# A hybrid decoder block on one core: Strassen operands paired in 1024-column tiles, a fifth raw buffer, and both norms' statistics and transposes reordered

## The chip, the cores and the metric

The kernel runs on one core of one Trainium2 chip. The metric is the device time of one execution in microseconds (us); the median of several runs counts. Four engines compute: TensorE (PE, with its weight loads written PEld), VectorE (DVE), ScalarE (ACT) and GpSimd (POOL). SyncE (SP) issues most of the DMAs. Each engine works through its own instructions in order; semaphores hold an instruction back until its inputs are there.

## The reference, cut to what matters

One layer of a decoder with 256 tokens, 2048 channels and a feed-forward width of 5632, all in float32:

```
mix = token_mixers(x, ...)                  # one input projection, gated linear attention,
                                            # forgetting attention, merge, output projection
x   = layer_norm(ALPHA*x + mix, ln1_g, ln1_b)
g   = causal_dwconv(x @ w_gate, conv_w, conv_b)
x   = layer_norm(ALPHA*x + (gelu(g) * (x @ w_up)) @ w_down, ln2_g, ln2_b)
x   = x + sigmoid(x @ w_ple_gate) * (p @ w_ple_proj)
```

The layer norm takes mean and variance over the 2048 channels of each token. The input spreads make the two norms' gains and biases about three times as wide as usual; that changes no operation.

## The kernel before, in words

**Weights.** All large weights come through one array, in units of 128 partitions x 2048 columns (1 MB), 284 in all. A unit is loaded as two "raw" tiles of 1024 columns (512 KB) by SP, into four raw buffers used in turn. Because TensorE multiplies in the shorter float32r format, each raw tile is split: ACT copies it to a "hi" tile, DVE subtracts to get the "lo" tile, and the product is summed from three matmuls (hi x hi, lo x hi, hi x lo, the activations being split likewise). There is a ring of six hi and one of six lo buffers. `unit()` (line 152) hands out the next unit and prepares up to three ahead; `prep()` (line 133) makes the loads and the splits.

**Order.** PE's and SP's order is the program's where the code says so; the order on DVE, ACT and POOL is set by a scheduler from priorities (`tc.high_priority`) and from when it expects inputs.

**The stages.** Input projections with attention beside them; the output projection with the residual and the first norm (`residual`, `end1`); gate and up projections with the convolution; the down projection `down` with the second norm (`end2`); the last gate (`begin2` and after).

**Down projection (dn).** It runs in two halves of 1024 output columns. Each half has 22 units, each a pair of 128-row weight blocks. Fourteen are "classic": 24 matmuls of 512 columns. Eight are done by a Strassen scheme (`strassen`, line 1079): seven products instead of eight, 21 matmuls. Their operands are the blocks b11, b21, b22 and four sums T1 = b12 - b11, T3 = b12 - b22, T2 = b22 - T1, T4 = b21 - T2 on DVE, each split into hi and lo (`prep_s`, line 110). b11 and each T get a hi and a lo tile of their own, 512 columns wide (`split512`); the second raw tile is split whole. So a Strassen unit takes six buffers of each ring, a classic unit two. They alternate through most of each half. A Strassen unit's products use them in the order b11, b21, b22, T1, T3, T2, T4. `fold` adds the product banks to the residual z when a half's Strassen units are done. At the end of a half `ev` adds the four result banks to z and takes the statistics of each 512-column group (bn_stats).

**The norms.** `ln_steps` (line 755) gives three steps for a half t of the tokens (128 each): `stat` (mean and rstd, with one power on POOL), `norm(g)` and `turn(g)` for each of four 512-column groups g. Groups 0 and 2 (`AFF_DVE`) have gain and bias applied by two DVE operations in `norm`, and `turn` transposes on PE and splits. Groups 1 and 3 are only normalised on ACT in `norm`; `turn` transposes, then applies gain and bias in four 128-column pieces, two on ACT and two on DVE, and then splits. For these groups the residual stream z itself gets gain and bias later, by `affine`, beside the next stage. `end1` interleaves by hand on PE: the last matmuls of the output projection, transposes, the first half of the per-layer-embedding projection (`proj`, whose result `put` copies and POOL stores), and the first three gate/up units (`phase0` with token half 0, `phase1` with half 1). `end2` does the same with the second half of that projection.

```
            tail_mm(1, 1, 0)
            turn0(0)
            tail_mm(1, 1, 1)
            stat1()
```

is the place in `end2` (lines 1147 to 1150) where the first transpose of the second norm stands. POOL's DMAs (two stores of z1, four of the embedding projection, two more) use a scratch of 8192 bytes for their descriptors.

Of the kernel before, what the change touches and what calls it, by code (L numbers as in the profile page):

```python
# [9 lines left out]
F32 = mybir.dt.float32  # L10
# [9 lines left out]
P = 128  # L20
# [13 lines left out]
P_STAT = 5000  # L34
P_LN1 = (2000, 2000)
P_LN2 = (4000, 1000)
# [6 lines left out]
            (0, 1, 2, 4, 3, 6, 5, 9, 7, 11, 8, 14, 10, 16, 12, 19, 13, 15, 17, 18, 20, 21))  # L43
AFF_DVE = (0, 2)
LN_ORDER = (1, 0, 3, 2)
# [7 lines left out]
def tile_block(ctx: ExitStack, tc: tile.TileContext, wu, wfv, wpp, xT_in, x_in, pT_in, wlr,  # L53
# [28 lines left out]
    def copy(o, i, scale=1.0):  # L82
        nc.scalar.activation(o, i, AF.Copy, bias=0.0, scale=scale)  # L83

# [17 lines left out]

    def split512(src, name):
        hi = ring.tile([P, 512], F32R, tag="hi", name=f"{name}h")
        copy(hi, src)
        lo = ring.tile([P, 512], F32R, tag="lo", name=f"{name}l")
        nc.vector.tensor_tensor(lo, src, hi.bitcast(F32), ALU.subtract)
        return hi, lo

    def prep_s(u):  # L110

        r0, r1 = [ring.tile([P, 1024], F32, tag="raw", bufs=4, name=f"raw{u}_{h}")
                  for h in range(2)]
        for h, r in enumerate((r0, r1)):
            nc.sync.dma_start(r, wu[u, :, h * 1024:(h + 1) * 1024])
        b12, b11, b22, b21 = r0[:, 0:512], r0[:, 512:1024], r1[:, 0:512], r1[:, 512:1024]
        ops = [split512(b11, f"b11_{u}")]
        hi = ring.tile([P, 1024], F32R, tag="hi", name=f"hi{u}_1")
        copy(hi, r1)
        lo = ring.tile([P, 1024], F32R, tag="lo", name=f"lo{u}_1")  # L120
        nc.vector.tensor_tensor(lo, r1, hi.bitcast(F32), ALU.subtract)
        ops += [(hi[:, 512:1024], lo[:, 512:1024]), (hi[:, 0:512], lo[:, 0:512])]
        ts = {}
        for n, a, b in (("T1", b12, b11), ("T3", b12, b22), ("T2", b22, "T1"),
                        ("T4", b21, "T2")):
            ts[n] = t2(f"{n}_{u}")
            nc.vector.tensor_tensor(ts[n], a, ts.get(b, b) if isinstance(b, str) else b,
                                    ALU.subtract)
        for n in ("T1", "T3", "T2", "T4"):
            ops.append(split512(ts[n], f"{n}_{u}"))  # L130
        ready[u] = ops

    def prep():
        u = n_prep[0]
        n_prep[0] += 1
        if u in dn_s:
            prep_s(u)
            return
        his, los = [], []
        for h in range(2):  # L140
            raw = ring.tile([P, 1024], F32, tag="raw", bufs=4, name=f"raw{u}_{h}")
# [4 lines left out]
            nc.vector.tensor_tensor(lo, raw, hi.bitcast(F32), ALU.subtract)  # L146
            his.append(hi)
            los.append(lo)
        ready[u] = (his, los)
# [45 lines left out]
    def load_consts2():  # L195
        nc.sync.dma_start(gnb, gnorm.broadcast_to([P, 512]))
        for i in range(2):
            maskf = ring.tile([P, 4, 256], F32, tag="raw", bufs=4, name=f"maskf{i}")
# [122 lines left out]
    def fv_prep(u, hs=(0, 1), his=None, los=None):  # L321
        his, los = his or [], los or []
        for h in hs:
            raw = ring.tile([P, NS], F32, tag="raw", bufs=4, name=f"fvraw{u}_{h}")
# [429 lines left out]

    def ln_steps(zof, stats, t, act_out, gb_, cg, cb, nm, prio):

# [11 lines left out]
        def norm(g):  # L768
            e = slice(g * 512, g * 512 + 512)
            zc = zof(t, g)  # L770
            with tc.high_priority(prio):
                if g in AFF_DVE:
                    nc.vector.scalar_tensor_tensor(zc, zc, mv[:, 0:1], gb_[0][:, e],
                                                   ALU.subtract, ALU.mult)
                    nc.vector.scalar_tensor_tensor(zc, zc, mv[:, 3:4], gb_[1][:, e],
                                                   ALU.mult, ALU.add)
                else:
                    nc.scalar.activation(zc, zc, AF.Identity, scale=mv[:, 3:4], bias=mv[:, 4:5])

        def turn(g):  # L780
            zc = zof(t, g)
            with tc.high_priority(prio):
                pt = mxtile(f"pt{nm}{t}{g}")
                for i in range(4):
                    nc.tensor.transpose(pt[:, i * P:i * P + P], zc[:, i * P:i * P + P], ident)
                if g in AFF_DVE:
                    split_T(pt, act_out[g], t)
                    return
                y = t2("lny").rearrange("p (k t) -> p k t", t=P)
                for i in range(4):  # L790
                    kt = 4 * g + i
                    gc, bc = chn[:, cg + kt:cg + kt + 1], chn[:, cb + kt:cb + kt + 1]
                    src = pt[:, i * P:i * P + P]
                    if i % 2 == 0:
                        nc.scalar.activation(y[:, i, :], src, AF.Identity, scale=gc, bias=bc)
                    else:
                        nc.vector.tensor_scalar(y[:, i, :], src, gc, bc, ALU.mult, ALU.add)
# [18 lines left out]

    def affine(zof, gb_, after, gs=range(4)):
        for t in range(2):
            for g in gs:
                zc = zof(t, g)  # L820
# [12 lines left out]
    def ple_prep(half):  # L833
# [4 lines left out]
        for k in range(2):  # L838
            raw = ring.tile([P, 1024], F32, tag="raw", bufs=4, name=f"praw{half}{k}")
            nc.sync.dma_start(raw, wpp[half, :, k * 1024:k * 1024 + 1024])  # L840
# [33 lines left out]
    def end1(tail_mm):  # L874
# [3 lines left out]
        with tc.manual_schedule(engines={mybir.EngineType.PE}):  # L878
# [8 lines left out]
            def put(t):  # L887
                for c in range(2):
                    o = t2("ppo")
                    copy(o, pb[t][c][0])  # L890
                    nc.gpsimd.dma_start(ppd[t, :, c * 512:c * 512 + 512], o)
# [13 lines left out]
            for c in range(2):  # L905
# [3 lines left out]
            (stat0, norm0, turn0), (stat1, norm1, turn1) = [  # L909
                ln_steps(z1of, st1, t, x1T, gain[0], c_g1, c_b1, "l1", P_LN1[t])  # L910
                for t in range(2)]
# [13 lines left out]
            turn0(G[2])  # L925
            proj(1, 0)
            put(0)
            for g in G[:2]:
                norm1(g)
            proj(0, 1)  # L930
            turn0(G[3])
            proj(1, 1)
            put(1)
            for i in range(3):
                phase0(i, slice(0, 12))
                turn1(G[i])
                if i == 0:
                    for g in G[2:]:
                        norm1(g)
            for i in range(3):  # L940
                phase0(i, slice(12, 16))
            for j in range(4):
                phase1(j)
                if j == 0:
                    turn1(G[3])
            first.extend(ps)

    residual("wo", mT, 16, z1, st1, (mid1, lambda: pq.append(ple_prep(0))), end=end1)
    mixers.append(affine(z1of, gain[0], lambda t: nc.gpsimd.dma_start(x1d[t], z1[t]),
                         [g for g in range(4) if g not in AFF_DVE]))  # L950

# [91 lines left out]
    pb, pq = [], []  # L1043

    def down(nh, tail, mid):

# [53 lines left out]
        def ev(t, c):  # L1100
            g = 2 * nh + c
            with tc.high_priority(P_STAT):
                nc.vector.tensor_tensor(z2of(t, g), z2of(t, g), C[t][c], ALU.add)
                nc.vector.bn_stats(st2[t][:, g, :], z2of(t, g))

# [23 lines left out]
    def end2(tail_mm):  # L1129
# [4 lines left out]
        with tc.manual_schedule(engines={mybir.EngineType.PE}):  # L1134
            for c in range(2):
                for i in range(2):
                    tail_mm(0, c, i)
            (stat0, norm0, turn0), (stat1, norm1, turn1) = [
                ln_steps(z2of, st2, t, x2T, gain[1], c_g2, c_b2, "l2", P_LN2[t])
                for t in range(2)]  # L1140
# [4 lines left out]
            for i in range(2):  # L1145
                tail_mm(1, 0, i)
            tail_mm(1, 1, 0)
            turn0(0)
            tail_mm(1, 1, 1)
            stat1()  # L1150
# [37 lines left out]
    mixers.append(affine(z2of, gain[1], lambda t: None,  # L1188
                         [g for g in range(4) if g not in AFF_DVE]))

# [122 lines left out]
```

## Time and profile before

| | |
|---|---|
| median of 3 runs | 1706.13 us (1703.06, 1706.13, 1709.03) |
| profiled execution | 1709.78 us, of which the profile's span is 1707.9 us |
| granted clock of TensorE | 0.999 |
| DVE, ACT busy | 1180.1 us (69%), 862.6 us (51%) |
| output projection's last unit to the first gate units (first norm) | about 845 to 885 us in the span |
| down projection | 1357.9 to 1604.3 us |
| last gate | from 1610.2 us |

A profile is one execution. Lines of the views name the kernel's line (L146), the engine, the tile written and the tiles read; numbers in tile names such as T_238 are the unit's. "<-" in a list of waits names what the waiting engine's instruction was released by. Start times are in us from the start of the span. Where PE is busy nearly throughout, time is to be found in the few places where it waits, and in why its operand is late there.

### The profile page before, as it was taken

The numbers are of one execution on the slowest core, as the hardware profiler recorded it, in microseconds if no ns is written. First come the engines' busy times: TensorE is split into PE (matmuls) and PEld (weight loads), VectorE is DVE, ScalarE is ACT, GpSimd is POOL, SyncE is SP. The second block draws the span as 40 slices with busy tenths as digits, with TensorE's granted clock in tenths as the row PEclk, the third lists the DMA queues.
The fourth block names the chain that finished last, engine by engine and source line by source line (L and its number), as shares of the span: only waits on it lengthen the run. The fifth ranks groups of instructions, "written<-read, shape, count | busy, mean of one in ns | idle before, by whom it ended". The sixth has DMA issues, their size and how long they took to land.

```text
span 1707.9 us, 23998 instructions
## 1 busy us (share of the span) xinstructions
PE 1691.3 (99%) x8987; PEld 1445.6 (85%) x8987; DVE 1180.1 (69%) x1762; ACT 862.6 (51%) x1264; POOL 35.7 (2%) x123
## 2 busy tenths in 40 slices
PE   9999999999999999999999999999999999999998
PEld 8888888888888888888788888888888887777787
DVE  6666668758756557774687777766666888778864
ACT  5745445445555544443365445544444555445543
POOL 1000000000000000000010000000000000000000
PEclk9999999999999999999999999999999999999999
DMA  9665555555555555657656665555556466576554
GB/s 314 227 190 165 164 185 173 181 176 173 178 177 164 172 187 189 190 187 280 208 180 191 213 213 191 187 189 189 188 186 192 154 215 197 173 248 228 183 175 164
DMA packets 91717, 330.24 MB, mean 193 GB/s; under 512 B 10264, under 2 KB 11936, under 8 KB 90448
## 3 DMA queue, kind: packets, MB, share of 16 engines
q1 hardware_dynamic: 90816, 324.51, 58.6%
q0 software_dynamic: 784, 4.20, 0.6%
q8 instruction: 70, 1.15, 0.3%
q14 instruction: 47, 0.39, 0.1%
HBM read 323.42 MB, written 5.25 MB: 192 GB/s over the span
## 4 chain that ended last, share of the span: by engine, by line
PE 85%; DMA 7%; DVE 5%; issue 1%; ACT 1%; SPq 0%; POOL 0%; ACTq 0%; DVEq 0%
PE psu L210 9%; PE psg L210 9%; PE psm L210 7%; DMA raw<-in_wu_dram 6%; PE gr L254 5%; PE gv L254 5%; PE psu L212 5%; PE psg L212 5%; PE pg L254 4%; PE psm L212 4%; PE psa L210 3%; PE wo L254 3%; PE dn L1065 3%; PE fv L354 2%; PE psa L212 2%; PE psfq L210 2%
## 5 line engine op out<-in xcount | busy, mean ns | idle before, releaser
L146 DVE TENSOR_TENSOR lo<-raw,hi 128x1024 fp32r<-128x1024 f32 x536 | 654.2, 1223 | 398.6 <-ACT hi L83 397.3
L83 ACT ACTIVATE hi<-raw 128x1024 fp32r<-128x1024 f32 x552 | 583.9, 1059 | 636.7 <-issue 254.4
L210 PE MATMUL psu<-x1T,hi 128*128 128x512 f32 x688 | 242.3, 393 | 0.0
L210 PE MATMUL psg<-x1T,hi 128*128 128x512 f32 x672 | 236.7, 393 | 0.0
L212 PE MATMUL psu<-x1T,lo 128*128 128x256 f32 x688 | 192.8, 280 | 0.0
L212 PE MATMUL psg<-x1T,lo 128*128 128x256 f32 x672 | 188.4, 280 | 0.0
L210 PE MATMUL psm<-xT,hi 128*128 128x512 f32 x512 | 180.1, 395 | 0.0
L210 PEld LDWEIGHTS psu<-x1T,hi 128*128 128x128 f32 x688 | 129.1, 188 | 29.6
L210 PEld LDWEIGHTS psg<-x1T,hi 128*128 128x128 f32 x672 | 126.1, 188 | 28.9
L212 PE MATMUL psm<-xT,lo 128*128 128x256 f32 x512 | 143.3, 280 | 0.0
L212 PEld LDWEIGHTS psu<-x1T,lo 128*128 128x128 f32 x688 | 129.6, 188 | 0.0
L212 PEld LDWEIGHTS psg<-x1T,lo 128*128 128x128 f32 x672 | 126.6, 188 | 0.0
L1065 PE MATMUL dn<-hi,hC 128*128 128x512 f32 x448 | 126.4, 394 | 0.0
L210 PEld LDWEIGHTS psm<-xT,hi 128*128 128x128 f32 x512 | 96.2, 188 | 21.6
L1065 PEld LDWEIGHTS dn<-hi,hC 128*128 128x128 f32 x448 | 84.1, 188 | 19.7
L212 PEld LDWEIGHTS psm<-xT,lo 128*128 128x128 f32 x512 | 96.5, 188 | 0.2
L210 PE MATMUL psa<-oT,hi 128*128 128x512 f32 x256 | 90.1, 393 | 0.0
L254 PE MATMUL gv<-hi,xT 128*128 128x512 f32 x256 | 73.6, 399 | 0.0
L254 PE MATMUL gr<-hi,xT 128*128 128x512 f32 x256 | 73.4, 399 | 0.0
L1065 PE MATMUL dn<-lo,hC 128*128 128x512 f32 x224 | 72.1, 397 | 0.9 <-DVE lo L146 0.9
L254 PE MATMUL wo<-hi,mT 128*128 128x512 f32 x256 | 71.9, 395 | 0.1
L212 PE MATMUL psa<-oT,lo 128*128 128x256 f32 x256 | 71.6, 280 | 0.0
(523 smaller groups left out, 2779.9 us busy)
## 6 DMA issues: line engine op xcount, KB each, us to landing
raw<-in_wu_dram SPq DMA_DIRECT2D x568, 512.0 KB, 4.4
fvraw<-in_wfv_dram SPq DMA_DIRECT2D x14, 524.0 KB, 5.9
lnb<-in_lng_dram SPq DMA_DIRECT2D x4, 1024.0 KB, 11.7
z<-in_x_dram SPq DMA_DIRECT2D x2, 1024.0 KB, 10.0
praw<-in_wpp_dram SPq DMA_DIRECT2D x4, 512.0 KB, 4.7
x1d<-z POOLq DMA_DIRECT2D x2, 1024.0 KB, 6.2
z<-x1d SPq DMA_DIRECT2D x4, 512.0 KB, 7.4
xraw<-in_xT_dram SPq DMA_DIRECT2D x7, 256.0 KB, 6.2
```

Source lines behind the costliest of these rows:

```text
L83: nc.scalar.activation(o, i, AF.Copy, bias=0.0, scale=scale)
L146: nc.vector.tensor_tensor(lo, raw, hi.bitcast(F32), ALU.subtract)
L210: nc.tensor.matmul(ps, lhsT=hi[i // 8 if hoff == 0 else 0][:, w0 % 1024:w0 % 1024 + P], rhs=a[:, kt % 4, :], start=first and i == 0, stop= ...
L212: nc.tensor.matmul(ps[:, 256:512], lhsT=lo[i // 8 if hoff == 0 else 0][:, w0 % 1024:w0 % 1024 + P], rhs=a[:, kt % 4, 0:256], start=False, ...
L254: nc.tensor.matmul(bs[j][:, 0:m], lhsT=x, rhs=v[:, o:o + m], start=first and i == 0, stop=last and i == 2)
L354: nc.tensor.matmul(fbk[t][c][:, 0:n], lhsT=x, rhs=w[:, o:o + n], start=kt == 0 and i == 0, stop=kt == 15 and i == 2)
L1065: nc.tensor.matmul(ps, lhsT=x, rhs=w, start=todo[id(ps)] == total[id(ps)], stop=todo[id(ps)] == 1)
```

## The change

- In a Strassen unit T1 and T3 share one 1024-column hi tile and one lo tile, T2 and T4 another pair; b11 has one whose second half is unused. The operations on them are the same.
- There are five raw buffers instead of four; POOL's descriptor scratch is 2048 bytes instead of 8192.
- In the first half of dn the four `bn_stats` leave `ev` and are issued in the second half, at its ninth unit; `ev` of the first half has no raised priority.
- In the first norm, token half 0 applies gain and bias ahead of the transpose in three groups (0, 2, 3); group 1's four pieces all go to ACT. Its priority rises from 2000 to 4000. `turn0` of the fourth group stands behind `proj(0, 1)` as before, but `put(0)` and the normalisation of half 1 now follow it; `put(1)` comes after the first `phase0`. `affine` does only the groups that were not done ahead.
- In the second norm the first transpose of half 0 moves from the middle of the tail's last bank to behind the first six projection matmuls, the second from behind twelve to behind eighteen.

```diff
-P_LN1 = (2000, 2000)
+P_LN1 = (4000, 2000)
...
-AFF_DVE = (0, 2)
+AFF1 = ((0, 2, 3), (0, 2))
+AFF2 = ((0, 2), (0, 2))
...
+    def pair512(a, b, name):
+        hi, lo = [ring.tile([P, 1024], F32R, tag=t, name=f"{t}{name}") for t in ("hi", "lo")]
+        out = []
+        for src, e in ((a, slice(0, 512)), (b, slice(512, 1024))):
+            if src is not None:
+                copy(hi[:, e], src)
+                nc.vector.tensor_tensor(lo[:, e], src, hi[:, e].bitcast(F32), ALU.subtract)
+                out.append((hi[:, e], lo[:, e]))
+        return out
...
-        r0, r1 = [ring.tile([P, 1024], F32, tag="raw", bufs=4, name=f"raw{u}_{h}")
+        r0, r1 = [ring.tile([P, 1024], F32, tag="raw", bufs=5, name=f"raw{u}_{h}")
...
-        ops = [split512(b11, f"b11_{u}")]
+        ops = pair512(b11, None, f"b11_{u}")
...
-        for n in ("T1", "T3", "T2", "T4"):
-            ops.append(split512(ts[n], f"{n}_{u}"))
+        ops += pair512(ts["T1"], ts["T3"], f"t13_{u}") + pair512(ts["T2"], ts["T4"], f"t24_{u}")
...
-                    if i % 2 == 0:
+                    if i % 2 == 0 or len(aff) == 3:
                         nc.scalar.activation(y[:, i, :], src, AF.Identity, scale=gc, bias=bc)
...
             proj(1, 0)
+            proj(0, 1)
+            turn0(G[3])
             put(0)
             for g in G[:2]:
                 norm1(g)
-            proj(0, 1)
-            turn0(G[3])
             proj(1, 1)
-            put(1)
             for i in range(3):
                 phase0(i, slice(0, 12))
                 turn1(G[i])
                 if i == 0:
+                    put(1)
...
-            with tc.high_priority(P_STAT):
+            with tc.high_priority(P_STAT if tail else 0):
                 nc.vector.tensor_tensor(z2of(t, g), z2of(t, g), C[t][c], ALU.add)
-                nc.vector.bn_stats(st2[t][:, g, :], z2of(t, g))
+                if tail:
+                    bn(t, g)
...
-            tail_mm(1, 1, 0)
-            turn0(0)
-            tail_mm(1, 1, 1)
+            for i in range(2):
+                tail_mm(1, 1, i)
...
-                if (k, t) == (1, 0):
+                if (k, t) == (0, 0):
+                    turn0(0)
+                elif (k, t) == (0, 1):
                     turn0(1)
...
     def late_loads():
+        for t in range(2):
+            for g in range(2):
+                bn(t, g)
...
-                     dynamic_dma_scratch_size=8192)
+                     dynamic_dma_scratch_size=2048)
```

More of the change, by code (lines that the diff above doesn't have):

```diff
@@ L82, in copy @@
     def copy(o, i, scale=1.0):
-        nc.scalar.activation(o, i, AF.Copy, bias=0.0, scale=scale)
+        return nc.scalar.activation(o, i, AF.Copy, bias=0.0, scale=scale)
     ctx.enter_context(tc.manual_schedule(engines={mybir.EngineType.SP}))
@@ L101, in tile_block @@
     ready = {}
[L103 to L108, printed above, removed]
+    def pair512(a, b, name):
[7 more added lines that the diff above has]
+        return out
     def prep_s(u):
-        r0, r1 = [ring.tile([P, 1024], F32, tag="raw", bufs=4, name=f"raw{u}_{h}")
+        r0, r1 = [ring.tile([P, 1024], F32, tag="raw", bufs=5, name=f"raw{u}_{h}")
                   for h in range(2)]
@@ L140, in prep @@
         for h in range(2):
-            raw = ring.tile([P, 1024], F32, tag="raw", bufs=4, name=f"raw{u}_{h}")
+            raw = ring.tile([P, 1024], F32, tag="raw", bufs=5, name=f"raw{u}_{h}")
             nc.sync.dma_start(raw, wu[u, :, h * 1024:(h + 1) * 1024])
@@ L197, in load_consts2 @@
         for i in range(2):
-            maskf = ring.tile([P, 4, 256], F32, tag="raw", bufs=4, name=f"maskf{i}")
+            maskf = ring.tile([P, 4, 256], F32, tag="raw", bufs=5, name=f"maskf{i}")
             nc.sync.dma_start(maskf, mask_in[:, 8 * i:8 * i + 8, :].rearrange(
@@ L323, in fv_prep @@
         for h in hs:
-            raw = ring.tile([P, NS], F32, tag="raw", bufs=4, name=f"fvraw{u}_{h}")
+            raw = ring.tile([P, NS], F32, tag="raw", bufs=5, name=f"fvraw{u}_{h}")
             hi = ring.tile([P, NS], F32R, tag="hi", name=f"fvhi{u}_{h}")
@@ L753, in tile_block, with ln_steps @@
     ppd = dr.tile([2, P, 1024], F32, name="ppd")
-    def ln_steps(zof, stats, t, act_out, gb_, cg, cb, nm, prio):
+    def ln_steps(zof, stats, t, act_out, gb_, cg, cb, nm, prio, aff):
         mv = sm.tile([P, 8], F32, tag="mv", name="mv")
@@ L771, in norm @@
             with tc.high_priority(prio):
-                if g in AFF_DVE:
+                if g in aff:
                     nc.vector.scalar_tensor_tensor(zc, zc, mv[:, 0:1], gb_[0][:, e],
@@ L785, in turn @@
                     nc.tensor.transpose(pt[:, i * P:i * P + P], zc[:, i * P:i * P + P], ident)
-                if g in AFF_DVE:
+                if g in aff:
                     split_T(pt, act_out[g], t)
@@ L815, in residual, with affine @@
                    end=end if nh == 1 else None)
-    def affine(zof, gb_, after, gs=range(4)):
+    def affine(zof, gb_, after, done):
         for t in range(2):
-            for g in gs:
+            for g in [g for g in range(4) if g not in done[t]]:
                 zc = zof(t, g)
@@ L838, in ple_prep @@
         for k in range(2):
-            raw = ring.tile([P, 1024], F32, tag="raw", bufs=4, name=f"praw{half}{k}")
+            raw = ring.tile([P, 1024], F32, tag="raw", bufs=5, name=f"praw{half}{k}")
             nc.sync.dma_start(raw, wpp[half, :, k * 1024:k * 1024 + 1024])
@@ L889, in put @@
                     o = t2("ppo")
-                    copy(o, pb[t][c][0])
+                    tc.keep_in_program_order(copy(o, pb[t][c][0]))
                     nc.gpsimd.dma_start(ppd[t, :, c * 512:c * 512 + 512], o)
@@ L909, in end1 @@
             (stat0, norm0, turn0), (stat1, norm1, turn1) = [
-                ln_steps(z1of, st1, t, x1T, gain[0], c_g1, c_b1, "l1", P_LN1[t])
+                ln_steps(z1of, st1, t, x1T, gain[0], c_g1, c_b1, "l1", P_LN1[t], AFF1[t])
                 for t in range(2)]
@@ L948, in tile_block @@
     residual("wo", mT, 16, z1, st1, (mid1, lambda: pq.append(ple_prep(0))), end=end1)
-    mixers.append(affine(z1of, gain[0], lambda t: nc.gpsimd.dma_start(x1d[t], z1[t]),
-                         [g for g in range(4) if g not in AFF_DVE]))
+    mixers.append(affine(z1of, gain[0], lambda t: nc.gpsimd.dma_start(x1d[t], z1[t]), AFF1))
     tc.keep_in_program_order(nc.scalar.preload_act_table_set("gelu_apprx_tanh_and_others"))
@@ L1043, in tile_block, with bn @@
     pb, pq = [], []
+    def bn(t, g):
+        nc.vector.bn_stats(st2[t][:, g, :], z2of(t, g))
     def down(nh, tail, mid):
@@ L1138, in end2 @@
             (stat0, norm0, turn0), (stat1, norm1, turn1) = [
-                ln_steps(z2of, st2, t, x2T, gain[1], c_g2, c_b2, "l2", P_LN2[t])
+                ln_steps(z2of, st2, t, x2T, gain[1], c_g2, c_b2, "l2", P_LN2[t], AFF2[t])
                 for t in range(2)]
@@ L1187, in tile_block @@
             copy(pp[1][:, t, c * 512:c * 512 + 512], pb[t][c][0])
-    mixers.append(affine(z2of, gain[1], lambda t: None,
-                         [g for g in range(4) if g not in AFF_DVE]))
+    mixers.append(affine(z2of, gain[1], lambda t: None, AFF2))
     def mid3():
```

## The prediction

> **What bounds the kernel now.** I read the page's first part, then the list of what TensorE (PE) waited for, then PE's busy time by stretch.
>
> ```profile
> PE 1691.3 (99%) x8987; PEld 1445.6 (85%) x8987; DVE 1180.1 (69%) x1762; ACT 862.6 (51%) x1264; POOL 35.7 (2%) x123
> ```
> PE is busy all but 16.6 us of the 1707.9 us span, and the change neither adds nor removes a matmul. So it can win PE's waits and no more. The list of waits (engine, what it waited for, us in total, times, longest) says where they are:
> ```profile
> PE dn L1065 <- DVE T_247l L107: 1.5, 1, 1.5
> PE ptl L785 <- DVE z L775: 1.2, 1, 1.2
> PE psg L223 <- DVE x1T L800: 1.1, 1, 1.1
> PE dn L1065 <- DVE lo L121: 0.9, 1, 0.9
> PE dn L1065 <- DVE lo L146: 0.9, 2, 0.6
> PE dn L1065 <- DVE T_238l L107: 0.8, 1, 0.8
> PE dn L1065 <- DVE T_261l L107: 0.8, 1, 0.8
> ```
> The rest is the fill at the start, the end, and smaller waits. Ten waits are in the down projection ("dn"), 6.6 us together, all for operand splits by VectorE (DVE) or ScalarE (ACT). One is at the second norm (ptl, 1.2), one at the first (psg, 1.1). By stretch (length, then PE busy, PEld busy, DVE busy, ACT busy, POOL busy, clock, DMA share, GB/s), the two halves of dn:
> ```profile
> 1358.00:1477.00 119.00, 117.59 (x505) 94.20 (x505) 97.19 (x136) 63.82 (x84) 0.00 (x0) 1.00 0.60 198
> 1477.00:1603.00 126.00, 119.47 (x505) 93.10 (x504) 100.92 (x135) 63.87 (x82) 1.00 (x1) 1.00 0.64 217
> ```
> No engine is full there; the clock is whole. The reason is order and latency, and DVE's timeline before one wait shows it:
> ```profile
> 1430.09 0.68 DVE L127 TENSOR_TENSOR T<-raw,T 128x512 f32<-128x512 f32 x1
> 1430.69 1.89 DVE L107 TENSOR_TENSOR T_238l<-T,T_238h 128x512 fp32r<-128x512 f32 x3
> 1436.06 0.69 DVE L127 TENSOR_TENSOR T<-raw 128x512 f32<-128x512 f32 x1 [3.48 <-DMA raw<-in_wu_dram]
> 1436.66 0.69 DVE L107 TENSOR_TENSOR T_238l<-T,T_238h 128x512 fp32r<-128x512 f32 x1
> ```
> The fourth T split of unit 238 stands behind the next Strassen unit's T1, which waits 3.48 us for its load; PE waits for that split at 1436.4.
>
> **What the dn waits cost.** An idle figure is too small, as PE refills after it. A Strassen unit and a classic unit (21 and 24 matmuls) take 10.45 us in the chain that ended last (1363.68 to 1374.13), 0.232 each. dn runs 2 x (14 x 24 + 8 x 21) = 1008 matmuls, 234.1 us. From its first start (1357.9) to the first matmul after it (1604.3) are 246.4 us. Of the 12.3 over, 0.4 is the transpose inside, 1.4 the wait at it; **10.5 us** is operand lateness. The Trainium skill (Perfetto Trace Analysis, Identifying the Most-Contended Engine) also calls matmul busy time a bad measure of headroom because matmuls are pipelined; by busy time alone this term would be 6.6.
>
> **Change 1: two operands to a tile, five raw buffers.** Nothing is added: per Strassen unit DVE has nine 512-wide operations (0.60 start to start) and one 1024-wide (1.14), 6.5 us; per classic unit two 1024-wide, 2.3: 8.8 of 10.45 us before and after. What moves is when a split may be written. There are six hi and six lo buffers. Before, a Strassen plus a classic unit take eight: T4 must wait until PE has left the classic unit just ahead, that is, until its own unit starts, and is read 18 matmuls = 4.2 us later. ACT 0.63 plus DVE 0.69 fit, but not with 3.48 us of waiting in the queue. After, the pair takes six, and each tile follows the same tile of the Strassen unit before: T2/T4's is free a classic unit (5.6 us) before its unit starts and is read 15 matmuls (3.5) later, 9.1 us in all.
>
> Does the queue still block? In the built order of the changed program DVE does all four T of the next Strassen unit, then the two lo of the classic unit before it, then that Strassen unit's splits. Count from PE's start on a Strassen unit: its successor's splits can end at 6.7 (its T2/T4 buffer is free at 4.9, ACT 0.6, DVE 2 x 0.6), the next four T at 9.1, the classic lo pair at about 10.3 and 12.7; PE reads them at 15.3 and 18.1. About 5 us are spare. Does the load keep up? With five buffers a Strassen unit's second load goes where the previous Strassen unit's first lay, free after its b11 split. The loop is load + three T (1.8) + two lo (2.28) + b11 lo (0.6) = load + 4.7, against 10.45: it keeps up while a load lands in **5.7 us**. Median landings in the stretches 1360 to 1420, 1420 to 1480, 1480 to 1600 are 5.0, 5.5 and 5.1. That is close; the 5 us spare covers single late ones (the longest is 11.2, beside the 2 x 1 MB gain load, which stays where it is).
>
> The bounds are 0 and all 10.5. I leave 1.5 (one late patch of about the size of those at 1437 or 1567): **-9.0**.
>
> **Change 2: first half's statistics later** (part of that -9.0). At 1480.72 DVE does four adds (2.4 us) and four statistics (2.4) ahead of T3, T2 and T4 of unit 247; PE idles 0.37 + 1.47. The statistics move among later units, where DVE has 1.6 us spare per pair; in the built order three adds go ahead of T2/T4's splits, 1.8 us, inside the 9.1. The adds also free the PSUM banks for unit 247 (needed 5.6 us after the half ends); if T3 of unit 249 waits for its load ahead of them they come by about 3.6. Cover: 2 us. Without it the wait stays, +1 to 2.
>
> **Change 3: first norm.** Group 3 of token half 0 goes from affine-after-transpose to the two 0.66 us DVE steps ahead; DVE gains 1.32 and loses four 0.33 (group 3's two, and group 1's two, now ACT's): zero. With the built order and the spacings of before, group 3's steps end on DVE at 856.4, PE turns it at 857.3, and its lo is written at 860.4 instead of 864.5. So the 1.07 wait at 864.58 goes. PE then runs on: first phase from 862.3, three times twelve matmuls (0.118 each) with three turns (0.36, one held 0.4 for its PSUM bank) and twelve more, to 869.6. There the second phase needs group 1 of half 1. Its lo stands on DVE behind half 0's last lo (863.7), four 1.14 weight splits, two 0.33 steps and a 0.60 lo: written by 870.1, against 870.7 before. That is what is late next: **-0.6**; bounds -1.2 (DVE ahead by half a microsecond) and +0.6 (ACT, with two more 0.44 steps, late). Of the moved copies, their four POOL DMAs (0.54 each) precede nothing on POOL until 883.6.
>
> **Change 4: second norm.** The first transpose moves behind the tail's last six matmuls and six of the projection, to about 1603.9; its z is written at 1602.3: the 1.4 goes. Then the next wait is half 1's first transpose. PE reaches it 1.4 earlier, after five gate matmuls, at 1610.0. Its z comes on DVE after the last add (from 1602.7): two 1.14 weight splits, a lo and a statistics step (0.60 each), four steps of 0.66 or less and the 0.5 on POOL, about 1609.7 to 1610.3. I give 0.3 back: **-1.1**; bounds -1.4 and 0.
>
> **The smaller scratch** (8192 to 2048) feeds POOL's DMAs: eight. The trace shows no wait for it, so: zero, or POOL held for a landing each (x1d 6.2, ppd 2.8) and the convolution's taps behind it: 2 x 6.2 at most. I take zero, nearest to the 0.54 an issue takes now. The Trainium skill (DMA: Bandwidth & Descriptors, The descriptor swizzle) gives nine descriptors per engine and side for 1 MiB, 16 bytes each (same page, Terms): an estimate of 144 bytes, far below 2048. By it the term is zero; no run shows it yet.
>
> **Sum.** -9.0 - 0.6 - 1.1 = -10.7. The profiled execution took 1709.78 (span 1707.9 plus 1.9), so 1699.1. That is 3.65 above the median 1706.13, and nothing shows whether those 3.65 are waits of the same kind (then the end stays 1699.1) or not (then 1695.4). I take **1698**, between the two and nearer the first, since late loads differ from run to run.
>
> **Rivals.**
> - Loads, not buffers, are late (22%). For: the chain through dn is 31% DMA. Then only the fifth buffer helps, about 1 us per load against T waits of up to 4.4 us; half of the 10.5 stays: 1698 + 5 = 1703, no difference to tell. Against: from 1000 to 1300 (5.6 us a unit) loads land in 4.3 with four buffers and PE never waits.
> - The raw loop becomes the bound: slower (8%). Five buffers put more loads in flight and each lands later. Decides at 5.7; at 7.1 each of 14 pairs loses 1.4, 19.6 less 5 spare is +14.6: 1698 + 15 = 1713. For: landings are at 5.0 to 5.5 and z loads at 7.1 to 7.7. Against: 198 to 217 GB/s against 383 in the best 10 us.
> - POOL is held by the scratch (3%): 1698 + 6 = 1704, as units of slack in gate/up cover half.
> - The change not doing what it says: the built order shows it does; it is within the first rival.
>
> **Numbers.** The forecast holds 67%, its own range 1693.5 to 1701. About 0.3% (5.1 us) is what a measurement of this kernel can tell from no change: faster is below 1701.0, slower above 1711.2. With a little of the first rival: faster 0.68, same 0.24, slower 0.08. The range takes in the first rival, the POOL case and the lower base: 1692.5 to 1706; above it lie the slow rival and a little more.
>
> **What would show it.** Right: PE's waits in dn fall from 6.6 us to 1.5 or less, none at unit 247; the psg wait at the first norm moves to x1T of half 1, about 0.5; the ptl wait is 0.5 or less. Wrong: T1/T3 on DVE still waiting 3 us or more for raw with PE waiting on a lo behind; raw landings over 5.7; POOL's x1d issue longer than 0.6.

## The result and the profile after

The changed kernel takes a median of **1697.55 us** (1697.30 to 1699.05, five runs), against 1706.13 (1703.06 to 1709.37, five runs) for the kernel before on the same chip: a ratio of **0.9949** with a 95% interval of 0.9932 to 0.9966. The forecast was 1698.0. The runs also lie closer together: 1.75 us apart instead of 6.3, and four of the five within 0.4.

The profiled execution is the slowest of the five, 1699.05 us with a span of 1697.2. The page's first part and the first line of its chain, by engine:

```profile
PE 1688.2 (99%) x8987; PEld 1448.1 (85%) x8987; DVE 1179.8 (70%) x1758; ACT 862.0 (51%) x1263; POOL 36.8 (2%) x123
...
PE 98%; DVE 1%; DMA 0%; SPq 0%; POOL 0%; issue 0%; ACT 0%
```

DVE's, ACT's and POOL's work is what it was, to about 1 us. PE idles 9.0 us of its span instead of 16.6. What ended last is now a chain of matmuls almost alone. The list of what PE waited for, complete (engine, what it waited for, us in total, times, longest):

```profile
PE fv L358 <- ACT fvhi L84: 1.5, 1, 1.5
PE warm_ps L94 <- DVE warm L91: 1.2, 1, 1.2
PE ptl L789 <- issue: 0.6, 1, 0.6
PE ptl L789 <- DVE lny L801: 0.4, 1, 0.4
PE psg L227 <- DVE x1T L804: 0.2, 1, 0.2
```

Here fv and psfq are the first projections' matmuls, warm_ps the very first ones, ptl the transposes of both norms, psg the gate projection behind the first norm, and pg (below) the last gate. No line of dn is left in it. The same by stretch (length, then PE, PEld, DVE, ACT and POOL busy, clock, DMA share, GB/s): the two halves of dn and the last matmuls before the last gate.

```profile
1358.00:1477.00 119.00, 119.00 (x516) 96.30 (x515) 100.89 (x143) 65.39 (x89) 0.00 (x0) 1.00 0.61 205
1477.00:1593.00 116.00, 116.00 (x501) 93.74 (x500) 97.13 (x129) 62.29 (x79) 1.00 (x1) 1.00 0.66 229
1593.00:1599.50 6.50, 6.50 (x34) 5.36 (x33) 6.06 (x12) 4.03 (x6) 0.99 (x1) 1.00 0.35 120
```

PE is busy for all of each. DVE still waits for its loads, as its timeline shows at the place that the prediction showed, the T splits of unit 238 and the next unit's T1 (start, length, operation, and in brackets the idle time ahead of it and what ended it):

```profile
1427.05 2.49 DVE L111 TENSOR_TENSOR lot<-T,hit 128x512 fp32r<-128x512 f32 x4
1431.58 0.69 DVE L132 TENSOR_TENSOR T<-raw 128x512 f32<-128x512 f32 x1 [2.05 <-DMA raw<-in_wu_dram]
1432.85 0.69 DVE L132 TENSOR_TENSOR T<-raw,raw 128x512 f32<-128x512 f32 x1 [0.57 <-DMA raw<-in_wu_dram]
...
1434.78 2.35 DVE L150 TENSOR_TENSOR lo<-raw,hi 128x1024 fp32r<-128x1024 f32 x2
```

and PE's timeline, where it comes to these splits:

```profile
1434.73 0.40 PE L1071 MATMUL dn_p<-hit,hS 128*128 128x512 f32 x1
1434.96 0.39 PE L1071 MATMUL dn_p<-lot,hS 128*128 128x512 f32 x1
...
1437.06 0.39 PE L1071 MATMUL dn<-lot,hS 128*128 128x512 f32 x1
...
1437.98 0.62 PE L1071 MATMUL dn<-lo,hC 128*128 128x512 f32 x2
```

All four splits now stand ahead of the T1 that waits. They are done at 1429.5; PE reads T1's at 1434.96 and the last at 1437.06, 5.4 and 7.5 us later. What stands behind that T1 now is the classic unit's lo: the first of the two is written by 1436.0 (1434.78 and the length of one, 1.22) and read at 1437.98, 2.0 us later.

Start to start, the 1699.05 compares with the 1709.78 of before as follows.

| stretch | before | after | difference |
|---|---|---|---|
| start to the first projection's matmul (psfq) | 52.9 | 54.7 | +1.8 |
| to the output projection (wo) | 712.3 | 712.2 | -0.1 |
| wo to its last matmul | 90.0 | 89.6 | -0.4 |
| first norm, gate and up, to dn | 502.7 | 502.3 | -0.4 |
| dn and second norm, to the last gate | 252.3 | 240.5 | -11.8 |
| last gate and end of span | 97.7 | 97.9 | +0.2 |
| span | 1707.9 | 1697.2 | -10.7 |

Most of the +1.8 in the first line is TensorE's clock in this one execution. PE's stretch from 14.2 to 17.6 us, in the profile after and in a second execution of the same kernel (E5 below):

```profile
14.20:17.60 3.40, 3.40 (x14) 3.40 (x13) 3.28 (x5) 2.58 (x3) 0.00 (x0) 0.51 1.02 416
14.20:17.60 3.40, 3.40 (x23) 3.40 (x23) 3.28 (x5) 2.74 (x4) 0.00 (x0) 1.00 1.01 416
```

PE is busy throughout in both, but at a granted clock of 0.51 it gets through 14 matmuls instead of 23. The same matmuls take 1.6 us longer than in E5 for that reason.

### The profile page after: what moved, and what is told of

It is laid out like the page before. It is cut to its first block, busy times and chain, and to the rows that moved or that the text cites. A ratio compares the mean times of both kernels' runs of the same rounds, so it can differ in the third digit from the quotient of the medians.

```text
span 1697.2 us, 23968 instructions
## 1 busy us (share of the span) xinstructions
PE 1688.2 (99%) x8987; PEld 1448.1 (85%) x8987; DVE 1179.8 (70%) x1758; ACT 862.0 (51%) x1263; POOL 36.8 (2%) x123
## 4 chain that ended last, share of the span: by engine, by line
PE 98%; DVE 1%; DMA 0%; SPq 0%; POOL 0%; issue 0%; ACT 0%
PE dn L1071 11%; PE psu L214 9%; PE psg L214 9%; PE psm L214 7%; PE gr L258 5%; PE gv L258 5%; PE pg L258 5%; PE wo L258 5%; PE psu L216 5%; PE psg L216 5%; PE psm L216 4%; PE psa L214 3%; PE dn_p L1071 3%; PE fv L358 2%; PE psa L216 2%; PE psfq L214 2%
```

## The experiments

Each group was run on one chip beside the kernel before, whose median there was 1710.5 (first group, E1 to E4), 1710.9 (E5 to E8) and 1710.2 (E9 to E12). "Lost in dn" is the length of dn less the 234.1 us of its 1008 matmuls, and less the transpose and what the ptl wait costs from start to start where these stand before dn's end; "idle" is the sum of PE's listed dn waits. Both are of one profiled execution each.

| | median us (range) | ratio (95%) | idle | lost in dn |
|---|---|---|---|---|
| before | 1706.13 (1703.06 to 1709.37) | | 6.6 | 10.5 |
| after | 1697.55 (1697.30 to 1699.05) | 0.9949 (0.9932 to 0.9966) | 0 | 0 |
| E1 after, unpaired | 1706.80 (1702.67 to 1708.73) | 0.9973 (0.9961 to 0.9985) | 5.5 | 9.7 |
| E2 after, 4 raw | 1699.35 (1697.54 to 1701.64) | 0.9934 (0.9921 to 0.9946) | 0 | 0 |
| E3 before, paired | 1702.99 (1699.70 to 1706.09) | 0.9954 (0.9941 to 0.9967) | 2.5 | 4.4 |
| E4 before, 5 raw | 1707.12 (1704.52 to 1709.81) | 0.9981 (0.9972 to 0.9990) | 5.7 | 8.1 |
| E5 after again | 1697.65 (1697.18 to 1699.39) | 0.9920 (0.9906 to 0.9933) | 0 | 0 |
| E6 statistics early | 1697.59 (1697.25 to 1697.80) | 0.9917 (0.9904 to 0.9931) | 0 | 0 |
| E7 first norm old | 1697.71 (1697.44 to 1697.99) | 0.9918 (0.9905 to 0.9932) | 0 | 0 |
| E8 second norm old | 1698.31 (1697.93 to 1698.43) | 0.9921 (0.9908 to 0.9935) | 0 | 0 |
| E9 4 raw, statistics early | 1699.31 (1697.60 to 1700.41) | 0.9940 (0.9926 to 0.9955) | 1.3 | 2.4 |
| E10 3 raw | 1730.16 (1727.98 to 1731.01) | 1.0120 (1.0105 to 1.0134) | 6.0 | 13.2 |
| E11 only T2/T4 paired | 1701.98 (1698.32 to 1702.76) | 0.9953 (0.9937 to 0.9968) | 0.6 | 0.9 |
| E12 4 raw, later transposes | 1697.84 (1697.04 to 1699.74) | 0.9932 (0.9920 to 0.9945) | 1.5 | 2.3 |

**E1, E3: the pairing taken away, and alone.** E1 is the changed kernel with

```diff
-        ops += pair512(ts["T1"], ts["T3"], f"t13_{u}") + pair512(ts["T2"], ts["T4"], f"t24_{u}")
+        for n in ("T1", "T3", "T2", "T4"):
+            ops.append(split512(ts[n], f"{n}_{u}"))
```

(and b11 likewise). E3 is the kernel before with the opposite edit and nothing else.

> The changed kernel with T1 to T4 again in a hi and a lo tile each; five raw buffers and all else kept. Theory 1 (a split is late because its buffer of the ring comes free late): the down projection takes 241 to 245 us instead of 234.1, with waits of PE for T splits back, and the time is 1704 to 1708. Theory 2 (the loads are late, the fifth raw buffer is what helped): the down projection stays at 234 to 236 us, the time at 1697 to 1699.

> The kernel before with only the pairing of T1 with T3 and T2 with T4 (four raw buffers, statistics early, both norms as before). Theory 1: the down projection's operand waits go but for unit 247's, 235 to 239 us plus the second norm's 1.4; time 1697 to 1701. Theory 2: no more than 2 us of the 10.5 go; time 1703 to 1707.

PE's dn waits in E1:

```profile
PE dn L1068 <- DVE lo L147: 1.6, 3, 0.5
PE dn L1068 <- DVE T_238l L108: 1.1, 1, 1.1
PE dn L1068 <- ACT T_261h L84: 1.0, 1, 1.0
PE dn L1068 <- DVE T_236l L108: 1.0, 1, 1.0
PE dn L1068 <- DVE T_261l L108: 0.8, 1, 0.8
```

and DVE's timeline at unit 238 in E1, where the order is that of before again:

```profile
1430.93 1.89 DVE L108 TENSOR_TENSOR T_238l<-T,T_238h 128x512 fp32r<-128x512 f32 x3
1435.85 0.69 DVE L128 TENSOR_TENSOR T<-raw 128x512 f32<-128x512 f32 x1 [3.03 <-DMA raw<-in_wu_dram]
...
1438.32 0.68 DVE L108 TENSOR_TENSOR T_238l<-T,T_238h 128x512 fp32r<-128x512 f32 x1
```

Three splits, then a T1 that waits 3.03 us for its load, then the fourth split: with everything else of the change in place, dn is 9.7 us too long again. Not all of that is late operands. From 1565.8 to 1569.2 the granted clock was 0.51 in this execution, and matmuls there start 0.43 us apart instead of 0.232; that is 1.5 of the 9.7, which leaves 8.2 of the 10.5. The run times agree: both E1's dn (243.8 us) and its median are in theory 1's ranges. So the buffers that the pairing saves are what lets the fourth split go ahead.

E3 shows the other side: alone, the pairing takes 10.5 to 4.4 in one execution, and no T split is among its dn waits, not even unit 247's. What is left are lo tiles of whole raw tiles (1.6 and 0.9); the first of them, at 1498.5, stands on DVE behind a T1 that waited 2.70 us for its load. That is more than theory 1 left: the median, 1702.99, is 2 us above its range and at theory 2's lower end, 7.5 us below the kernel before on that chip, where the whole change was worth about 13 on another (E5). The pairing is the largest part, and not all of it.

**E2, E4: the fifth buffer taken away, and alone.**

```diff
-            raw = ring.tile([P, 1024], F32, tag="raw", bufs=5, name=f"raw{u}_{h}")
+            raw = ring.tile([P, 1024], F32, tag="raw", bufs=4, name=f"raw{u}_{h}")
```

is E2, in all places that name this ring; E4 is the kernel before with the opposite and the scratch of 2048.

> The changed kernel with four raw buffers instead of five. Theory 1 (ring buffers): the down projection stays at 234 to 236 us and the time at 1696 to 1699. Theory 2 (loads): 239 to 245 us, time 1702 to 1707. Beside that, the start: if the fifth buffer is what made the first projection end 1.8 us later than before (psfq from 54.7 instead of 52.9), it starts at about 52.9 here; if that was chance, it can be anywhere from 52.9 to 54.7.

> The kernel before with only the fifth raw buffer and the scratch of 2048 bytes that pays for it. Theory 1: operand waits of 7 to 11 us stay in the down projection; time 1704 to 1708. Theory 2: half or more of them go; time 1697 to 1701. If the fifth buffer delays the start, psfq starts at about 54.7, and POOL's two x1d issues stay at 0.54 us if the scratch costs nothing.

In E2's execution dn loses nothing; its median, 1699.35, is a little above theory 1's range. In E4's the waits are those of the kernel before (T splits and lo), and 8.1 us are lost; its median is 3.4 us below the kernel before. The rival "loads, not buffers, are late" falls as the main cause: a buffer more for the loads gives 2.4 of 10.5, and the pairing with four buffers leaves 0, 2.4 and 2.3 us (E2, E9, E12).

What E2 loses lies outside dn. The output projection (wo to its last matmul) takes 91.0 us instead of 89.6, with a wait of 0.8 for z, and the second norm's ptl wait is 1.2 instead of 0.6. Wo takes 89.6 in all eight profiled executions with five buffers and 89.8 to 91.0 in the five with four, the kernel before among them: the -0.4 of that line of the table belongs to the fifth buffer.

**E5 to E8: the smaller parts undone one at a time.**

> The changed kernel again, as the reference for the other three on the same chip. Both theories: ratio to before 0.993 to 0.996; dn 234.1 to 234.6 us long with at most 0.3 us of operand waits; first norm's psg wait 0.2 to 0.4, second norm's ptl wait 0.4 to 0.7. If the first projection (psfq) starts at 54 to 55 us in the span again, its later start belongs to the change; if at 52.9 to 53.7, it was chance.

E5 is the changed kernel without an edit. Its dn is 234.1, and psfq starts at 53.3; in E6 to E8 at 53.1 to 53.4. The +1.8 us of the table's first line are of that one execution. The ratio, 0.9920, is below the range expected of it: the changed kernel's median is the same on this chip to 0.1 us, the kernel before's is 4.8 higher.

E6 has the statistics of the first half back in `ev`, at the raised priority:

```diff
-            with tc.high_priority(P_STAT if tail else 0):
+            with tc.high_priority(P_STAT):
...
-                if tail:
-                    bn(t, g)
+                bn(t, g)
```

> The changed kernel with the four statistics of the first half back in ev at raised priority (one part undone). Theory 1 (a split's early buffer gives 9.1 us of cover, so the statistics no longer matter once the operands are paired): no wait at unit 247 or at most 0.3 us, dn within 0.4 us of the changed kernel's. Theory 2 (the statistics are a cost of their own, the eight DVE operations in a row hold the splits back whatever the buffers are): the waits at unit 247 are back, 1 to 1.9 us, dn 1.3 to 2.2 us longer.

DVE's timeline of E6 at the end of the first half:

```profile
1471.81 0.69 DVE L132 TENSOR_TENSOR T<-raw 128x512 f32<-128x512 f32 x1 [4.40 <-DMA raw<-in_wu_dram]
...
1474.16 0.69 DVE L111 TENSOR_TENSOR lot<-T,hit 128x512 fp32r<-128x512 f32 x1
1474.76 2.47 DVE L1109 TENSOR_TENSOR z<-z,dn 128x512 f32<-128x512 f32 x4
1477.15 2.46 DVE L1049 BATCH_NORM_STATS2 st<-z 128x6 f32<-128x512 f32 x4
1479.53 1.88 DVE L111 TENSOR_TENSOR lot<-T,hit 128x512 fp32r<-128x512 f32 x3
```

All eight operations stand in a row ahead of three T splits, after a load that held DVE for 4.40 us, and PE waits for none of it. With paired operands and five buffers the move of the statistics is worth nothing: theory 2 falls.

E7 has the first norm as it was:

```diff
-P_LN1 = (4000, 2000)
+P_LN1 = (2000, 2000)
...
-AFF1 = ((0, 2, 3), (0, 2))
+AFF1 = ((0, 2), (0, 2))
```

and the old places of `put` and `norm1`.

> The changed kernel with the first norm as it was (groups 0 and 2 affine ahead in both token halves, the old order of the projection and the copies, the old priority). Theory 1 (the norm's change is worth its own 0.5 to 0.6 us and independent of the rest): the psg wait for half 0's x1T is back at 0.9 to 1.2 us in place of 0.2, from the output projection's end to the first gate and up units 0.4 to 0.7 us more. Theory 2 (the time from there is set by half 1's operand, so that the order of half 0 is worth nothing): no more than 0.2 us of difference in that stretch.

PE's timeline at the norm in E7:

```profile
864.53 0.74 PE L227 MATMUL psg<-x1T,hi 128*128 128x256 f32 x4 [1.09 <-DVE x1T L804]
```

and in E5:

```profile
867.86 0.66 PE L789 MATMUL ptl<-ident,z 128*128 128x128 f32 x4 [0.38 <-DVE lny L801]
870.19 0.39 PE L227 MATMUL psg<-x1T,hi 128*128 128x256 f32 x1 [0.24 <-DVE x1T L804]
```

One wait of 1.09 for half 0 comes back in place of 0.38 for a PSUM bank and 0.24 for half 1. From wo's end to dn are 502.7 us instead of 502.3 in E5, E6 and E8: 0.4, as theory 1 had it. The run times do not resolve it: the medians of E5 to E7 are within 0.12 us.

E8 has the second norm's transposes where they stood:

```diff
-            for i in range(2):
-                tail_mm(1, 1, i)
+            tail_mm(1, 1, 0)
+            turn0(0)
+            tail_mm(1, 1, 1)
...
-                if (k, t) == (0, 0):
-                    turn0(0)
-                elif (k, t) == (0, 1):
+                if (k, t) == (1, 0):
                     turn0(1)
```

> The changed kernel with the second norm's two transposes where they stood before. Theory 1 (the wait at the first transpose is worth 1.1 to 1.4 and 0.3 to 0.6 of it comes back at half 1's first transpose): ptl wait of 1.1 to 1.4 us before the tail's end, none or at most 0.2 at half 1's transpose, the last gate starts 0.6 to 1.0 us later against the down projection's start. Theory 2 (z is there earlier now, since the dn operands no longer delay DVE): the ptl wait is below 0.5, and the move was worth nothing.

PE's timeline there in E8:

```profile
1591.13 0.66 PE L789 MATMUL ptl<-ident,z 128*128 128x128 f32 x4 [1.06 <-DVE z L779]
```

The wait is back, and the 0.6 at half 1's first transpose is gone. The last gate starts 1.3 us later after dn's start (241.8 for 240.5) and is 0.8 shorter (90.4 for 91.2): 0.5 us in all. The waits are as theory 1 had them. Its 0.6 to 1.0 is met at neither place: 1.3 at the gate's start, 0.5 at its end. The medians differ by 0.66 (1698.31 against 1697.65).

**E9: four raw buffers and early statistics together,** the edits of E2 and E6.

> The changed kernel with four raw buffers and with the first half's statistics early again: the two parts of which either alone could be undone without a wait in dn. Theory A (with pairing each of the two covers for the other: eight DVE operations in a row put DVE behind, and with four buffers the loads that start later keep it behind): 1.5 to 3 us of operand waits in dn's second half, on the classic units' lo, dn 237 to 240 us long, as in the kernel before with pairing alone. Theory B (pairing alone is enough, the 2.5 us left there were late loads by chance): at most 0.5 us of waits, dn 234 to 235.

The loss, 2.4 us, and the idle time, 1.3, lie between the two theories' numbers, and the run times are those of E2 (1699.31 against 1699.35). So the early statistics do not add to what four buffers leave, and E9 doesn't tell the theories apart. In E9 and E12 one of PE's waits is for the lo of a Strassen unit's second raw tile (0.6 and 0.7 us), and that lo stands on DVE behind a T1 that waited 3.84 and 3.90 us for its load. Dn lost 0, 2.4 and 2.3 us in the three executions with the pairing and four buffers (E2, E9, E12), and nothing in after and E5 to E8 with five. The medians of the three are 1699.35, 1699.31 and 1697.84, against 1697.55 to 1697.71 in after and E5 to E7: the fifth buffer is worth up to 1.8 us, and the runs with it lie closer together (0.5 to 2.2 us against 2.7 to 4.1). These are medians of different chips, and the intervals of the ratios overlap, so the size is not clear of the noise.

**E10: three raw buffers,** `bufs=3` in the place of E2's edit.

> The changed kernel with three raw buffers. The prediction's rival 'the raw loop becomes the bound' in a form that must bind if its sum is right: with three buffers a buffer goes round in three tiles of four per pair, so 3/4 x 10.45 = 7.84 us for a landing, a wait in DVE's queue and the operations on it; at a landing of 5 us only 2.8 are left, and a Strassen unit's second tile alone has two lo (2.3) and up to four T ahead of it. Theory 1: the loop binds in dn, 12 to 45 us of operand waits, and little elsewhere (5.6 us a unit, 8.4 a buffer's round, one split of about 2.2 on it). Theory 2 (loads land sooner when fewer are under way, 3.5 to 4 us, so that even three are enough): dn below 240.

The longest waits of PE in E10:

```profile
PE psg L227 <- ACT hi L84: 3.9, 1, 3.9
PE pl L473 <- DVE fk L241: 3.4, 1, 3.4
PE ptl L789 <- issue: 2.1, 1, 2.1
PE dn L1071 <- DVE lo L126: 2.0, 4, 0.8
PE dn_p L1071 <- ACT hib L84: 1.8, 1, 1.8
```

The program is 30 us of span longer than E5. Dn has 13.2 of them, from 6.0 us of idle time, below what theory 1 expected; wo has 5.5, the stretch from the first norm to dn 5.2, the projections 3.6 and the rest about 3. That other stages would lose little was wrong. The two longest waits are outside dn: PE stands 3.95 us at 879.78, at the first gate units behind the first norm, for a hi copy which on ACT had itself waited for a raw load, and 3.4 in the attention. Part of the 13.2 is the clock's: from 1553.6 to 1560.6 the granted clock was 0.51, and ten matmuls there start 0.43 us apart instead of 0.232, at least 1.9 us. That leaves at most 11.3 for late operands, just under theory 1's 12. Two more such stretches, 853.8 to 857.4 and 877.6 to 884.6, are inside the losses of wo and of the first norm. Fewer loads did land sooner, 4.4 to 4.5 us in dn, and it didn't help.

**E11: half of the pairing.**

```diff
-        ops += pair512(ts["T1"], ts["T3"], f"t13_{u}") + pair512(ts["T2"], ts["T4"], f"t24_{u}")
+        ops += pair512(ts["T1"], None, f"t1_{u}") + pair512(ts["T3"], None, f"t3_{u}") + pair512(ts["T2"], ts["T4"], f"t24_{u}")
```

> The changed kernel with only T2 and T4 in one tile, T1 and T3 in a tile each: seven buffers of each ring for a Strassen and a classic unit instead of six (before: eight). T2/T4's tile is then the first of the classic unit before, free 12 matmuls (2.8 us) ahead of its unit and read 15 matmuls (3.5) after its start: 6.3 us of cover, between 4.2 and 9.1. Theory 1 (the waits go by cover): nearly all gone, 0 to 1.5 us of waits, dn 234.1 to 236.5. Theory 2 (what counts is that the ring turns exactly once per pair, so that a tile always follows itself and never stands behind the unit just ahead): about half of the unpaired kernel's 5.5 us and more is left, 2.5 to 6, dn 238 to 244.

The profiled execution meets theory 1: one wait of 0.6 us in dn, 0.9 lost. But it is the fastest of four runs (1698.32); the others took 1701.39 to 1702.76, some 4 us above E5, which are theory 2's numbers. One can't say which from a trace of the good run alone. The medians are in order of cover, 4.2 us (E1, 1706.8), 6.3 (1702.0), 9.1 (E5, 1697.65), and that much is consistent with either; what the slower three of E11 waited for stays open.

**E12: a candidate.** Four raw buffers, and the second norm's half 1 transposed behind the 12th and 24th matmul of the last gate:

```diff
-            turn1(0)
...
-                    if t == 0 and i == 0:
-                        turns[1](1)
+                    if t == 0:
+                        turns[1](i)
```

> A candidate: the changed kernel with four raw buffers and the second norm's first transpose of half 1 moved from the fifth to behind the twelfth matmul of the last gate, its second behind the 24th. The 0.6 us wait on ptl goes if it is only the transpose's place: 0.6 to 0.9 us less from dn's start to the last gate's end, median 1696.5 to 1698 on a chip where the changed kernel takes 1697.6. Rival: half 1's x2T then comes late for the second token half (needed 5.6 us after the gate's start, written about 5.4 after it), a new wait of 0.3 to 1 us on pg, and nothing is gained.

The ptl wait on issue is gone, no pg wait has come, and the last gate takes 90.4 us instead of 91.2. The 0.8 is there, and the four buffers lose 2.3 in dn in the same execution: 1697.84, no better than the changed kernel. The later transposes with five buffers weren't tried.

## Why the prediction was right, point by point

- **What bounds the kernel.** Right: what was won is PE's waits, and those in dn were the most of it (E1: with the rest of the change, unpaired, 8.2 us of lateness remain). The list of parts was one short: the 0.4 in wo that came with the fifth buffer is in no term.
- **Dn, -9.0.** The mechanism was right and the size was short: -10.5, since the 1.5 left for a late patch are in none of five executions with the pairing and five buffers (after, E5 to E8). The queue did still block as counted (T1 waits 2.05 us in the profile after, 4.40 in E6). The spare counted as about 5 us was for the classic unit's lo; in the profile after that lo came 2.0 us ahead of PE, behind DVE's waits of 2.05 and 0.57, which is 4.6 without them. (In that count the second lo should end at 11.4, one step of 1.14 behind 10.3, and not at 12.7; the first one sets the spare.) Reading the loss from start to start and not from busy time made this term right, but "PE refills after it" is only part of the reason. A matmul is recorded 0.39 to 0.40 us long, while starts stand 0.232 apart, so the first 0.16 of a delay leaves no idle time; and the matmul behind the late one starts 0.34 later. That makes about 0.27 us a wait on top of what the list shows: E11's one wait has 0.64 idle and 0.9 lost, E12's three 1.5 and 2.3, the ten of before 6.6 and 9.3, and the other 1.1 or so of before are delays too short to be listed.
- **Load keeps up while it lands in 5.7.** Medians in dn were 4.8 to 5.6 after and 5.2 to 5.3 in E5, so the rival of the raw loop did not come. That the loop can bind is shown with three buffers (E10), not the point from which it would with five.
- **Statistics later, as a part.** "Without it the wait stays, +1 to 2" is a step that was wrong, read as a statement on the move: E6 leaves the move out and loses nothing. The wait at unit 247 went with the pairing (E3 has no wait for a T split either).
- **First norm, -0.6.** 0.4 by the table of stretches and by E7. The two waits named as next are there: 0.37 for the PSUM bank (0.4 expected), 0.24 for half 1's x1T (0.5 expected).
- **Second norm, -1.1.** By the table of stretches -11.8 + 0.2 + 10.5 = -1.1; undone by itself (E8) only 0.5 in the profile and 0.66 in the medians, so the term was about twice too large. The gain up to the gate is 1.3 in E8, near the 1.4. The size that was off is what is given back: the wait at half 1 is 0.57 (0.5 or less expected) and costs 0.8, which E8 and E12 both have back, not 0.3. In the table this is hidden, as the kernel before had a wait of its own in the last gate, 0.3 on a lo, that the changed kernel doesn't have.
- **Scratch, zero.** Right. POOL's timeline has the x1d issue in the kernel before:

```profile
961.88 0.54 POOL L949 DMA_DIRECT2D x1d<-z  x1 [8.63 <-DVE z L822]
```

and both of them after:

```profile
940.28 0.54 POOL L953 DMA_DIRECT2D x1d<-z  x1 [8.72 <-DVE z L826]
985.78 0.54 POOL L953 DMA_DIRECT2D x1d<-z  x1 [9.53 <-DVE z L826]
```

An issue takes 0.54 us with either scratch, and POOL is held by DVE's z alone. The estimate from the Trainium skill's count of descriptors (DMA: Bandwidth & Descriptors, The descriptor swizzle) gave zero for this term too, and the trace agrees: 0.54 us an issue.
- **The base.** The sum of 1699.1 and the profiled 1699.05 agree, but by luck: dn gave 1.5 more and wo 0.4 more, the first norm 0.2 less, and the fill took 1.8 more, which E5 to E8 show to be of that execution. The typical changed run is the span of E5, 1695.8, which is 12.1 below the profiled run before. The forecast of 1698 came near the median because it started close to that profiled run and the gain was larger than the sum. Whether before's 3.65 us over its median were waits of the same kind is what the scatter speaks to: it fell from 6.3 us to 1.75, and the end stayed near 1697.6 on both chips while before's median went from 1706.13 to 1710.9. That speaks for it; no trace of one of before's faster runs shows it. The end at 1695.4 was not reached by any run.

## What to carry to other kernels

Where operands go through a ring of buffers and one engine prepares them in order, count for each tile when its buffer comes free and when it is read: the difference is the cover for everything that can stand in that engine's queue. Putting two half-width operands into one full tile raised this cover from 4.2 to 9.1 us without an instruction more, and made a late load, which still comes, invisible. Read the loss from start to start of the matmuls, since each wait here cost about 0.27 us more than the idle time that the list gives it, and look at the granted clock of the same stretch before calling the whole loss late operands (E1, E10). Look at the scatter of the runs too: a profile is one execution, and E11's was the fastest of four, after's the slowest of five.

## What the runs showed of the hardware

**Landings.** In dn the landing of a 512 KB load was longer with more raw buffers, that is, with more loads that can be under way. With the pairing the medians are 4.5 us with three buffers (E10), 4.8 to 5.0 with four (E2, E3, E9, E12) and 5.0 to 5.3 with five (after, E5 to E8); unpaired they are 5.2 with four (before) and 5.3 and 5.5 with five (E1, E4). From 1000 to 1300 us, in the gate and up projections, there is no such order: 4.1 with three, 4.0 to 4.7 with four, 3.5 to 4.8 with five, and two executions of the same changed kernel have 3.5 (after) and 4.7 (E5). So the number of buffers isn't all of it, and the prediction's rival had the sign for dn alone; the size, a few tenths, is what it lacked.

**The clock.** In three of the fourteen profiled executions, and apart from the last few us of the span, the granted clock falls to about half for 3.4 to 7.0 us: in after from 14.2 (0.51), in E1 from 1565.8 (0.51), in E10 at the three places named (0.51 to 0.53). In dn, matmuls that start 0.232 us apart otherwise start 0.43 apart there. PE had waited 1.5 us or more, in one wait or two, in the 4 us before each. But fill waits of 1.5 to 1.8 us in E3, E4 and E8, and the 0.37 and 1.47 at unit 247 in the kernel before, were not followed by one, so what sets it off stays open.
